# Hybrid decoder layer on one core: the weight tile's load issued ahead of the sum of w_ada and its load, in each step

## Chip, cores and metric

The kernel runs on 1 core of one Trainium2 chip. The metric is the device time of one execution in microseconds. Engines are PE (TensorE matmul, with PEld for its weight loads), DVE (VectorE), ACT (ScalarE), POOL (GpSimd) and SP (SyncE, which here issues all loads and stores, in one queue).

## What is computed

One decoder layer for x of 256 x 4096 in float32. Cut to what matters here:

```python
mod = jax.nn.silu(c) @ w_ada + b_ada             # c: 4096, w_ada: 4096 x 12288
shift, scale, gate = jnp.split(mod, 3, axis=-1)
h = rms_norm(x, norm_g) * (1 + scale[:, None, :]) + shift[:, None, :]
z = h @ w_in                                      # w_in: 4096 x 15520
...
yA = rms_norm(yA, out_norm_a_g) * jax.nn.silu(gA)
yB = rms_norm(yB, out_norm_b_g) * jax.nn.silu(gB)
y = jnp.concatenate([yA, yB], axis=-1) @ w_out    # w_out: 4096 x 4096
return x + gate[:, None, :] * y
```

Between the two products stand a spatial gating branch (yA) and a sparse attention branch (yB), both fed from z.

## The kernel before

**Steps.** All of `w_in` and `w_out` passes through one list, `stream`, of 624 steps. A step is a weight tile of 2 x 128 rows and mostly 512 columns (512 KB, name `raw`). For each step `load_w` (L400) issues the tile's load on SP, three steps ahead (`AHEAD` = 3) into one of four buffers (`WBUFS` = 4). `split` (L412) then cuts the tile into a high half `whi`, written by ACT (L419), and the rest `wlo` = raw - whi, of whose 1024 columns POOL writes 704 (L427, in two pieces) and DVE 320 (L425). `multiply` (L430) issues 10 or 12 matmuls of 512 columns (L457). A buffer of `raw` is free when ACT, POOL and DVE have read it.

**Chunks.** The rows of `w_in` come in eight chunks of 512, 46 steps each, for the columns in `early`: steps 0 to 367. After them come the columns of the two gate paths (128 steps) and `w_out` (128 steps). At the end of each visit of two steps DVE adds the product to what is there (`add_to`, L829), 1024 elements wide.

**The sums of w_ada.** A chunk can be multiplied only once h is known for its rows, and h needs scale and shift: `silu(c) @ w_ada`. The first chunk's share is made before step 0 (`first_ada`). The other seven are made beside the steps: `ada_gemv` (L181) takes a tile `wa` of 128 x 1024 (512 KB), multiplies it by a column of silu(c) and adds it to `acc` on DVE (L196, L194 for the first of a chunk), and then calls `load_ada` (L165), which issues the load of the next tile (L178) into the one of two `wa` buffers that this sum has just freed. `pace` (L1016) says in how many steps such a sum stands: it spreads the 33 turns of a chunk (32 sums, and one that hands `acc` to ACT) evenly over the columns that PE has to multiply until the chunk is due. It is called in steps 0 to 321 alone; in later steps sums of w_ada for the gate come from `tick` (called inside `step`, L463).

**Order.** The program runs under `manual_schedule`: each engine gets its instructions in the order in which the loop writes them. In a step t below 322 that is: `pace` (DVE's sum, then SP's `wa` load, which waits for it), then `step`: SP's load of the weight tile of step t + 3, `split`, the reading of products, `tick`, `multiply`.

Of the kernel before, what the change touches and what calls it, by code (L numbers as in the profile page):

```python
# [37 lines left out]
AHEAD = 3  # L38
# [4 lines left out]
def layer(ctx, tc, x, c, w_ada, b_ada, norm_g, w_in, ln_v_g, ln_v_b, w_s, b_s, q_norm_g,  # L43
# [25 lines left out]
    def flush():  # L69
        while pending:  # L70
            pending.pop(0)()
# [290 lines left out]
    def tick():  # L362
        small_ones[0] = 0
        for b in list(beside):
            b[2] += b[1]
        for b in list(beside):
            if small_ones[0] > 1:
                break
            again = False
            while b[2] >= 1.0:  # L370
                b[2] -= 1.0
                if again:
                    flush()
                again = True
                if next(b[0], "end") == "end":
                    beside.remove(b)
                    break
# [22 lines left out]
    def load_w(t):  # L400
        if t >= len(stream) or t in raws:
            return
        v, i = stream[t]
        nk, w, c0 = min(2, len(v["ks"]) - i), v["w"], v["c0"]
        raw = wp.tile([P, 2, 512], F32, name="raw")
        raw = raw[:, :nk]
        nc.sync.dma_start(raw[:, :, :w], v["src"][:, v["ks"][i]:v["ks"][i] + nk, c0:c0 + w])
        raws[t] = raw
# [3 lines left out]
    def split(t):  # L412

        raw, w = raws.pop(t), stream[t][0]["w"]
        nk = raw.shape[1]
        hi = [sp.tile([P, 512], F32R, name="whi") for _ in range(nk)]
        lo = [sp.tile([P, 512], F32R, name="wlo") for _ in range(nk)]
        for kk in range(nk):
            nc.scalar.activation(hi[kk][:, :w], raw[:, kk, :w], AF.Copy)  # L419
        left = nk * pool_cols[0] * w // 1024 * 2  # L420
        for kk in range(nk):
            cut = w - min(left, w)
            left -= w - cut
            if cut:
                nc.vector.tensor_sub(lo[kk][:, :cut], raw[:, kk, :cut], hi[kk][:, :cut].bitcast(F32))  # L425
            if cut < w:
                nc.gpsimd.tensor_sub(lo[kk][:, cut:w], raw[:, kk, cut:w], hi[kk][:, cut:w].bitcast(F32))  # L427
        halves[t] = hi, lo

    def multiply(t):  # L430

        v, i = stream[t]
        hi, lo = halves.pop(t)
        if i == 0:
            if v is visits[-1]:
                v["ps"] = [misc() for _ in range(NT)]
            else:
                both = mm.tile([P, NT, 512], F32, name="mm_ps", tag="mm")
                v["all"], v["ps"] = both, [both[:, n] for n in range(NT)]
        (ah, al), w, ks = v["parts"], v["w"], v["ks"][i:i + len(hi)]  # L440

        def half(a, k, n):
            return a[k][:, n * P:(n + 1) * P]
        todo = []
        for k, b in zip(ks, hi):
            if v["packed"]:
                todo += [(0, h_both[k], b), (1, half(ah, k, 1), b), (1, half(al, k, 1), b)]
            else:
                todo += [(n, half(a, k, n), b) for a in (ah, al) for n in range(NT)]
        for k, b in zip(ks, lo):  # L450
            todo += [(n, h_both[k] if v["packed"] and n == 0 else half(ah, k, n), b) for n in range(NT)]
        if t + 1 == len(stream):
            todo.sort(key=lambda x: x[0])
        ends = {n: max(j for j, x in enumerate(todo) if x[0] == n) for n in range(NT)}
        begun = set() if i == 0 else {0, 1}
        for j, (n, a, b) in enumerate(todo):
            nc.tensor.matmul(v["ps"][n][:, :w], a, b[:, :w], start=n not in begun,  # L457
                             stop=i + len(hi) == len(v["ks"]) and j == ends[n])
            begun.add(n)
# [1 line left out]
    reads = []  # L461

    def step(t):  # L463
        load_w(t + AHEAD)
        due = [v for u, v in reads if u <= t]
        del reads[:len(due)]
        split(t)
        flush()
        for v in due:
            v["read"](v)  # L470
        v, i = stream[t]
        if i == 0 and v["before"]:
            v["before"]()
        tick()
        multiply(t)
        if i + 2 >= len(v["ks"]):
            reads.append((t + 2, v))
# [538 lines left out]
    def pace(t):  # L1016
        nonlocal steps, owed
        cols = until[t + 1] - until[t]
        owed += max([((KC + 1) * b - steps) * cols / max(until[max(at[b] - LEAD, 0)] - until[t], cols)
                     for b in range(1, len(BLOCKS)) if (KC + 1) * b > steps] + [0.0])  # L1020
        while owed >= 1.0:
            owed -= 1.0
            steps += 1
            next(hs, None)
# [37 lines left out]
    with tc.manual_schedule():  # L1062
        for t in range(len(stream)):
            for begin in start.get(t, ()):
                begin()
            if t < last:
                pace(t)
            elif t == last:
                pool_cols[0] = POOL_REST
            step(t)  # L1070
        for _, v in reads:
            v["read"](v)
# [42 lines left out]
```

## Time and profile before

| | |
|---|---|
| median of 3 runs | 1890.69 us (1889.44 to 1894.2) |
| the profiled execution | 1893.78 us, its span 1892.1 us |
| granted TensorE clock over the span | 0.994 |
| PE matmul busy | 1809.0 us (96%) |
| PE weight loads busy | 1439.2 us (76%) |
| DVE busy | 1443.7 us (76%) |
| ACT busy | 933.4 us (49%) |
| POOL busy | 1299.2 us (69%) |
| moved by DMA | 542.53 MB, mean 287 GB/s |

Busy times are of one profiled execution. A matmul is drawn from its start to a modelled end, and the next one starts before that end, so PE's busy time is not the time that it needs. SP only issues and waits; its instructions are not counted as busy. Idle time of an engine is put down to what ended it.

### The profile page before, as it was taken

How to read it: one execution, taken by the hardware profiler on the slowest of the kernel's cores; microseconds unless marked ns; L12 is line 12 of the kernel's file. 1: busy time of each engine (PE TensorE's matmuls, PEld its weight loads, DVE VectorE, ACT ScalarE, POOL GpSimd, SP SyncE). 2: the span in 40 equal slices, each digit the busy share in tenths (PEclk: the TensorE clock that was granted, in tenths of full speed). 3: DMA queues.
4: the chain of work that ended last, by engine and by line, in shares of the span. 5: the costliest groups of instructions: out<-in, count | busy, mean ns of one | idle time of the engine just before them, and what ended most of it. 6: DMA issues, size and time to landing. Idle time of an engine off the chain costs nothing.

```text
span 1892.1 us, 27366 instructions
## 1 busy us (share of the span) xinstructions
PE 1809.0 (96%) x8100; PEld 1439.2 (76%) x8100; DVE 1443.7 (76%) x1600; ACT 933.4 (49%) x1716; POOL 1299.2 (69%) x1340
## 2 busy tenths in 40 slices
PE   5798999999999999999999999999999999999998
PEld 2476777777777777787788877788888888888877
DVE  4656788888888888888777888887887577677744
ACT  4356445445454354444455556567654554544443
POOL 0366777777777776777785545767667777877786
PEclk9899999999999999999999999999999999999999
DMA  9899999999999989999975467886788799899974
GB/s 319 316 340 323 314 317 316 318 324 309 341 320 333 319 300 315 329 301 322 311 210 152 132 206 257 267 264 202 245 281 303 248 332 339 294 318 343 320 216 154
DMA packets 269550, 542.53 MB, mean 287 GB/s; under 512 B 17270, under 2 KB 25688, under 8 KB 269404
## 3 DMA queue, kind: packets, MB, share of 16 engines
q1 hardware_dynamic: 269404, 540.79, 84.5%
q8 instruction: 66, 1.08, 0.2%
q14 instruction: 80, 0.66, 0.1%
HBM read 536.51 MB, written 4.22 MB: 286 GB/s over the span
## 4 chain that ended last, share of the span: by engine, by line
PE 45%; DVE 2%; DMA 1%; POOL 1%; ACT 1%; issue 1%; SPq 0%; DVEq 0%; POOLq 0%; ACTq 0%
PE mm_ps L457 38%; PE ms_ps L457 2%; PE ms_ps L573 1%; DMA raw<-in_w_in_dram 1%; DVE wlo L425 1%; PE ms_ps L714 0%; DVE acc L196 0%; POOL wlo L427 0%; PE ms_ps L915 0%; PE ms_ps L867 0%; DVE v L809 0%; PE ms_ps L556 0%; PE ms_ps L742 0%; ACT whi L419 0%; DVE ix L585 0%
## 5 line engine op out<-in xcount | busy, mean ns | idle before, releaser
L427 POOL TENSOR_TENSOR wlo<-raw,whi 128x512 fp32r<-128x512 f32 (+1 forms) x1248 | 1220.8, 1004 | 543.8 <-ACT whi L419 467.0
L419 ACT ACTIVATE whi<-raw 128x512 fp32r<-128x512 f32 (+1 forms) x1248 | 730.9, 618 | 829.9 <-DMA raw<-in_w_in_dram 385.1
L425 DVE TENSOR_TENSOR wlo<-raw,whi 128x320 fp32r<-128x320 f32 (+2 forms) x624 | 636.7, 1022 | 317.3 <-ACT whi L419 200.9
L457 PE MATMUL mm_ps<-whi,hh 128*128 128x512 f32 (+1 forms) x1728 | 566.2, 397 | 19.2 <-ACT whi L419 15.5
L457 PE MATMUL mm_ps<-whi,hl 128*128 128x512 f32 (+1 forms) x1728 | 550.7, 388 | 2.6 <-DVE hl L311 2.6
L457 PE MATMUL mm_ps<-wlo,hh 128*128 128x512 f32 (+1 forms) x1728 | 494.0, 388 | 14.3 <-DVE wlo L425 12.2
L196 DVE SCALAR_TENSOR_TENSOR acc<-wa,csil,acc 128x1024 f32<-128x1024 f32 x341 | 436.4, 1280 | 72.3 <-DMA wa<-in_w_ada_dram 71.2
L457 PEld LDWEIGHTS mm_ps<-whi,hh 128*128 128x128 f32 x1728 | 315.2, 190 | 97.2 <-ACT whi L419 31.0
L457 PEld LDWEIGHTS mm_ps<-wlo,hh 128*128 128x128 f32 x1728 | 320.4, 189 | 86.3 <-POOL wlo L427 12.0
L457 PEld LDWEIGHTS mm_ps<-whi,hl 128*128 128x128 f32 x1728 | 323.8, 189 | 71.0 <-DVE hl L311 2.9
L457 PE MATMUL mm_ps<-whi,yh 128*128 128x512 f32 x448 | 138.1, 389 | 0.0
L457 PE MATMUL mm_ps<-whi,yl 128*128 128x512 f32 x448 | 138.0, 389 | 0.0
L457 PE MATMUL mm_ps<-wlo,yh 128*128 128x512 f32 x448 | 120.2, 390 | 0.6 <-POOL wlo L427 0.6
L457 PE MATMUL mm_ps<-wlo,both 128*128 128x512 f32 x256 | 103.9, 406 | 4.3 <-DVE wlo L425 3.0
L457 PE MATMUL mm_ps<-whi,both 128*128 128x512 f32 x256 | 103.8, 405 | 3.9 <-ACT whi L419 2.8
L457 PEld LDWEIGHTS mm_ps<-wlo,yh 128*128 128x128 f32 x448 | 83.9, 188 | 19.0 <-POOL wlo L427 1.8
L457 PEld LDWEIGHTS mm_ps<-whi,yl 128*128 128x128 f32 x448 | 84.1, 188 | 17.6
L457 PEld LDWEIGHTS mm_ps<-whi,yh 128*128 128x128 f32 x448 | 84.0, 188 | 17.6 <-ACT whi L419 0.2
L457 PEld LDWEIGHTS mm_ps<-wlo,both 128*128 128x128 f32 x256 | 48.0, 187 | 30.7 <-POOL wlo L427 14.5
L829 DVE TENSOR_TENSOR qi<-qi,mm_ps 128x1024 f32<-128x1024 f32 x56 | 67.6, 1207 | 0.0
L457 PEld LDWEIGHTS mm_ps<-whi,both 128*128 128x128 f32 x256 | 48.0, 188 | 23.9 <-ACT whi L419 11.1
L217 PE MATMUL acc<-wa,csil 128*1 128x512 f32 x64 | 28.4, 613 | 10.9 <-DMA wa<-in_w_ada_dram 10.9
(190 smaller groups left out, 1035.5 us busy)
## 6 DMA issues: line engine op xcount, KB each, us to landing
raw<-in_w_in_dram SPq DMA_DIRECT2D x480, 512.0 KB, 5.9
wa<-in_w_ada_dram SPq DMA_DIRECT2D x384, 512.0 KB, 5.0
raw<-in_w_out_dram SPq DMA_DIRECT2D x128, 512.0 KB, 6.0
xs<-in_x_dram SPq DMA_DIRECT2D x8, 512.0 KB, 5.5
xres<-in_x_dram SPq DMA_DIRECT2D x8, 512.0 KB, 7.3
out_dram<-yt SPq DMA_DIRECT2D x16, 256.0 KB, 3.1
raw<-in_w_in_dram SPq DMA_DIRECT2D x16, 160.0 KB, 5.1
wk<-rb_d SPq DMA_DIRECT2D x16, 128.0 KB, 5.6
```

Of the source, the lines that this page charges most:

```text
L196: nc.vector.scalar_tensor_tensor(dst, src, csil[:, k:k + 1], dst, op0=OP.mult, op1=OP.add)
L217: nc.tensor.matmul(acc[g:g + 1, s, :w], csil[:, k:k + 1], wt[:, s], start=i < 4, stop=i >= KC // 2 - 4)
L419: nc.scalar.activation(hi[kk][:, :w], raw[:, kk, :w], AF.Copy)
L425: nc.vector.tensor_sub(lo[kk][:, :cut], raw[:, kk, :cut], hi[kk][:, :cut].bitcast(F32))
L427: nc.gpsimd.tensor_sub(lo[kk][:, cut:w], raw[:, kk, cut:w], hi[kk][:, cut:w].bitcast(F32))
L457: nc.tensor.matmul(v["ps"][n][:, :w], a, b[:, :w], start=n not in begun, stop=i + len(hi) == len(v["ks"]) and j == ends[n])
L573: nc.tensor.matmul(dots[:q, a * S:(a + 1) * S], qt[:, (h0 + a) * q:(h0 + a + 1) * q], kiT[:, :S], start=True, stop=True)
L829: nc.vector.tensor_add(z, z, p)
```

## The change

The call of `load_w` moves out of `step` and into the loop, ahead of `pace`. In a step t the load of the weight tile of step t + 3 is now written before DVE's sum of w_ada and before the load into the buffer that the sum frees.

```diff
@@ def step(t):
-        load_w(t + AHEAD)
         due = [v for u, v in reads if u <= t]
@@ with tc.manual_schedule():
             for begin in start.get(t, ()):
                 begin()
+            load_w(t + AHEAD)
             if t < last:
                 pace(t)
```

SP's queue in steps 148 to 152, before. `raw` are weight tiles (L407), `wa` tiles of w_ada (L178); the numbers are the buffers' names in the build.

```order
L407 DMA raw_4341<-in_w_in_dram 128x2x512
L178 DMA wa_4366<-in_w_ada_dram 128x2x512
L407 DMA raw_4368<-in_w_in_dram 128x2x512
L178 DMA wa_4393<-in_w_ada_dram 128x2x512
L407 DMA raw_4395<-in_w_in_dram 128x2x512
L407 DMA raw_4417<-in_w_in_dram 128x2x512
L178 DMA wa_4440<-in_w_ada_dram 128x2x512
L407 DMA raw_4442<-in_w_in_dram 128x2x512
L178 DMA wa_4467<-in_w_ada_dram 128x2x512
L407 DMA raw_4469<-in_w_in_dram 128x2x512
```

Here each `wa` load stands ahead of the weight load of its step: raw_4395 comes behind wa_4393, which waits for a sum. The same place on SP with the change:

```order
L407 DMA raw_4341<-in_w_in_dram 128x2x512
L407 DMA raw_4365<-in_w_in_dram 128x2x512
L178 DMA wa_4368<-in_w_ada_dram 128x2x512
L407 DMA raw_4392<-in_w_in_dram 128x2x512
L178 DMA wa_4395<-in_w_ada_dram 128x2x512
L407 DMA raw_4417<-in_w_in_dram 128x2x512
L407 DMA raw_4439<-in_w_in_dram 128x2x512
L178 DMA wa_4442<-in_w_ada_dram 128x2x512
L407 DMA raw_4466<-in_w_in_dram 128x2x512
L178 DMA wa_4469<-in_w_ada_dram 128x2x512
```

Each weight load has moved ahead of its step's `wa` load: raw_4392 is the former raw_4395, and wa_4395 the former wa_4393. DVE's queue at the same place, before; the change leaves its order as it is.

```order
L425 TENSOR_TENSOR wlo_4373<-raw_4294,whi_4371 128x320
L829 TENSOR_TENSOR qi1_168<-qi1_168,mm_ps_4305 128x1024
L196 SCALAR_TENSOR_TENSOR acc_3834<-wa_4317,csil_160,acc_3834 128x1024
L425 TENSOR_TENSOR wlo_4400<-raw_4319,whi_4398 128x320
L425 TENSOR_TENSOR wlo_4422<-raw_4341,whi_4420 128x320
L829 TENSOR_TENSOR v2_177<-v2_177,mm_ps_4352 128x1024
L196 SCALAR_TENSOR_TENSOR acc_3834<-wa_4366,csil_160,acc_3834 128x1024
```

The subtraction that reads raw_4294 is DVE's last use of the buffer that raw_4395 goes into. The sum of wa_4317, two rows on, is what the load of wa_4393 waits for; before, raw_4395 stood behind that wait, and with the change it does not.

## Rows read from the trace of the kernel before

**Rows 1.** Busy by stretch: us, busy us (x) of PE PEld DVE ACT POOL, PEclk, DMA share, GB/s

```profile
64.00:206.00 142.00, 126.00 (x541) 100.23 (x542) 92.24 (x105) 79.82 (x132) 91.99 (x95) 0.95 0.90 311
206.00:962.00 756.00, 730.34 (x3212) 574.23 (x3211) 631.84 (x639) 342.65 (x620) 560.17 (x564) 1.00 0.92 316
...
1500.00:1600.00 100.00, 100.00 (x451) 82.98 (x450) 77.30 (x73) 46.74 (x81) 72.95 (x74) 1.00 0.93 324
```

**Rows 2.** The chain that ended last, 1500 to 1660: start us, us, what

```profile
1502.24 43.54 PE mm_ps L457 x192
```

**Rows 3.** PE's groups by shape, 206 to 962: xcount | busy us, mean ns | idle before

```profile
L457 PE MATMUL mm_ps<-whi,hh 128*128 128x512 f32 x864 | 287.6, 396 | 13.9 <-ACT whi L419 12.4 <-DVE u L829 0.4 <-DVE v L829 0.4
...
L457 PE MATMUL mm_ps<-whi,both 128*128 128x512 f32 x192 | 77.7, 405 | 3.9 <-ACT whi L419 2.8 <-DVE v L829 0.8
L263 PE MATMUL ms_ps<-one,accs 128*128 128x1 f32 x96 | 11.0, 245 | 0.0
...
L457 PE MATMUL mm_ps<-whi,hh 128*128 128x160 f32 x48 | 9.1, 270 | 0.0
```

**Rows 4.** Waits of ACT and of DVE, 206 to 962: total us, times, longest

```profile
ACT whi L419 <- DMA raw<-in_w_in_dram: 302.7, 155, 5.0
...
DVE wlo L425 <- ACT whi L419: 90.7, 99, 3.1
DVE acc L196 <- DMA wa<-in_w_ada_dram: 29.5, 35, 3.0
```

**Rows 5.** SP's own waits, 206 to 962: total us, times, longest

```profile
SPq L178 <- DVE acc L196: 264.4, 131, 4.5
SPq L178 <- DVE wlo L425: 111.4, 47, 4.2
SPq L178 <- DMA wa<-in_w_ada_dram: 78.2, 81, 3.8
...
SPq L407 <- POOL wlo L427: 30.8, 74, 1.2
```

**Rows 6.** DMA, 206 to 930: GB/s in 40 slices; loads, KB, median us to landing

```profile
GB/s 322 342 336 314 308 294 324 331 315 333 307 321 298 309 354 321 356 324 339 298 299 345 327 320 332 333 280 308 322 321 298 316 344 297 301 315 324 317 328 340
...
raw<-in_w_in_dram SPq DMA_DIRECT2D x254, 512.0 KB, 6.3
wa<-in_w_ada_dram SPq DMA_DIRECT2D x183, 512.0 KB, 5.3
```

**Rows 7.** Timeline at 490 us, SP, DVE, POOL, ACT: start us, us, what, idle before

```profile
491.67 0.37 SPq L178 DMA_DIRECT2D wa<-in_w_ada_dram  x1
492.13 0.93 SPq L407 DMA_DIRECT2D raw<-in_w_in_dram  x2
...
495.71 0.42 SPq L407 DMA_DIRECT2D raw<-in_w_in_dram  x1
...
489.24 1.21 DVE L829 TENSOR_TENSOR qi<-qi,mm_ps 128x1024 f32<-128x1024 f32 x1
490.37 1.27 DVE L196 SCALAR_TENSOR_TENSOR acc<-wa,csil,acc 128x1024 f32<-128x1024 f32 x1
...
493.94 1.28 DVE L196 SCALAR_TENSOR_TENSOR acc<-wa,csil,acc 128x1024 f32<-128x1024 f32 x1
...
487.67 2.10 POOL L427 TENSOR_TENSOR wlo<-raw,whi 128x512 fp32r<-128x512 f32 x2 [1.54 <-ACT whi L419]
490.44 6.24 POOL L427 TENSOR_TENSOR wlo<-raw,whi 128x512 fp32r<-128x512 f32 x6 [0.66 <-ACT whi L419]
...
489.73 2.44 ACT L419 ACTIVATE whi<-raw 128x512 fp32r<-128x512 f32 x4 [1.62 <-DMA raw<-in_w_in_dram]
...
497.95 2.45 ACT L419 ACTIVATE whi<-raw 128x512 fp32r<-128x512 f32 x4 [2.92 <-DMA raw<-in_w_in_dram]
```

**Rows 8.** First chunk, 64 to 206: DVE's waits; loads, KB, median us to landing

```profile
DVE acc L196 <- DMA wa<-in_w_ada_dram: 32.5, 26, 3.4
...
wa<-in_w_ada_dram SPq DMA_DIRECT2D x41, 512.0 KB, 4.5
```

## Prediction

> **What bounds the kernel now.** I cut the span where one part of the program ends and the next begins, because the change acts in one part alone: `pace` runs only in steps 0 to 321, which are seven chunks of 46 steps. The view of busy time by stretch comes first [rows 1]. The first chunk takes 142 us (64 to 206), the next six, 276 steps, 756 us (206 to 962). The reader should see that in those six no resource stands out: PE is busy 730 of 756 us, DVE 632, and the DMA engines 0.92 of the time.
>
> PE's busy figure hides loss, since each matmul is drawn longer than the distance to the next. That distance is read from an undisturbed stretch late in the kernel: 43.54 us for 192 matmuls, 0.2268 us each [rows 2]. Against it stands a drawn duration of 0.40 us [rows 3]. So I price PE's work by the distance. The 512-column matmuls of the six chunks (three kinds of 864, two of 192; one of each is shown) are 2976 x 0.2268 = 675 us. The 144 narrow ones (three kinds of 48) are drawn 0.27 us long; less the same tail of 0.17 us that is 0.10 us each, 15 us by estimate. The 96 small ones that sum the modulations are 11 us [rows 3]. PE's floor is 701 us, so **55 us, 9 us a chunk, are lost to waiting**. That is the whole prize in these six chunks.
>
> Who is late? The waits of the same stretch [rows 4]: ACT waited 302.7 us, 155 times, for the weight tile `raw`; DVE waited 90.7 us for ACT's half `whi`, and only 29.5 us for a `wa` tile. So the weight tile comes late and ACT late behind it, and what multiplies comes late behind ACT.
>
> Why is it late? SP's own waits say it [rows 5]: SP stood 264.4 + 111.4 + 78.2 = 454 us in front of the `wa` load (L178), against 30.8 us for POOL in front of the weight load (L407). Over 183 `wa` loads [rows 6] that is 2.5 us each, and the weight load stands behind in the same queue. The stretch at 490 us shows one case in full [rows 7]. POOL's pair that ends at 489.77 is the last reader of a weight buffer; nothing else keeps the next load. But DVE first does an addition of 1.21 us and then the sum of `wa` from 490.37 to 491.64; SP issues `wa` at 491.67 and the weight tile at 492.13, 2.36 us late. That tile is the one for which ACT then sits idle 2.92 us before 497.95. In the next case POOL's second pair after that is done at about 494.6 (490.44 plus two thirds of 6.24), the sum at 495.22, and the weight load goes out at 495.71, 1.1 us late: here the sum came before the addition could. So a weight load loses about 1.1 us, or 2.4 us where an addition stands between, in each step that has a sum.
>
> **The change part by part.** *Moved:* in steps 0 to 321 the weight load of step t+3 goes ahead of the sum, and so of the `wa` load, of step t. No instruction is added or removed, and DVE's order is the same. From step 322 on nothing stands between the old place and the new.
>
> *What the weight loop gains.* Four buffers make a loop of four steps: landing 6.3 us [rows 6], then the use of the tile (from ACT's start at 489.73 to POOL's end at 492.5, a third of the way through its six: 2.8 us [rows 7]), then the delay of the next issue. At 756/276 = 2.74 us a step the loop has 10.96 us; 6.3 + 2.8 leave 1.9 us for the delay and rests, which agrees with 1.1 to 2.4 us in two steps of three. Without the delay the loop is 9.1 us, 2.28 us a step, below PE's floor of 701/276 = 2.54 us. The weight loop then no longer sets the pace.
>
> *What is late next.* First PE itself, at 701 us. Second the DMA: it moved 316 GB/s on average in the six chunks [rows 1], in slices of 18 us between 280 and 356 [rows 6]. At PE's floor the same bytes need 316 x 756/701 = 341 GB/s, a rate that only the best slices have. Third DVE: 632 us of work and 29.5 us of waits for `wa` fit into 701 us, but closely.
>
> *The wait that is added.* SP now waits for the weight buffer (POOL's subtraction, above all) with the `wa` load queued behind, and DVE's sum waits for what that brings. In both cases of rows 7 POOL was done before the sum was (489.77 against 491.64, 494.6 against 495.22), so `wa` would go out when it does now. I take 0; the upper bound is what POOL's wait costs the weight load now, 30.8/74 = 0.4 us each [rows 5]. The loop of the two `wa` buffers is 5.3 us of landing [rows 6] and 1.3 us of sum [rows 7], 6.6 us for two loads, where 756 us and 183 loads give 8.3 us and PE's floor 7.7 us. Neither bound eats that room of 1.1 us.
>
> *The first chunk.* DVE waits 32.5 us for `wa` in its 142 us, more than in the six others together, with 41 loads [rows 8]. There the `wa` loop sets the pace, and an earlier weight tile brings little. I take 0, between 10 us gained (7%, as the six would at PE's floor) and the loss that the third rival prices.
>
> *Sum.* The six chunks can give 0 (the DMA holds its rate) to 55 us (PE's floor). I take 30, somewhat over half. The nearest stretch argues for the upper part: from 1500 to 1600 us, where a step's weight load already goes before its sum, PE is busy 100 of 100 us with the DMA at 324 GB/s [rows 1]. But PE's floor would need 5% more than that rate, and waits for `wa` grow with it. A gain of 30 us means 726 us at 329 GB/s. The profiled execution took 1893.8 us, so it becomes 1863.8; the median of the runs shown is 3.1 us lower, and I forecast **1861 us**.
>
> **The rivals.**
>
> *PE's floor is reached* (chance 0.17). All waits behind weights vanish, 55 us: 1836 us. For it speaks the late stretch; against it the rate of 341 GB/s.
>
> *Nothing moves* (0.13). The transfer is hidden anyway: the DMA engines are busy 0.92 of the time already, and a load issued 2 us sooner only lies longer in the queue; or its own buffer is the true gate and the change does not do what it says. Time 1891 us. Against it: slices of 345 and 356 GB/s in the same stretch [rows 6] show room, and rows 7 show the buffer free while SP stood elsewhere.
>
> *The `wa` tile becomes the late one* (0.08). Of two loads issued 0.46 us apart the second lands after 6.3 us and the first after 5.3 [rows 6, 7]: being second costs 1.0 us. If the two simply swap, the `wa` loop grows from 6.6 to 7.6 us for two. In the six chunks that is about PE's floor of 7.7, and since DVE does nothing else while it waits for a sum, I give them no gain. In the first chunk, which waits for `wa` already, 41 loads in two buffers lose 0.5 us each, 20 us: 1891 + 20 = 1911 us. It decides from the point at which `wa` lands 0.5 us or more later, 5.8 us, and the six chunks gain less than the first loses; beyond 7.0 us (8.3 less 1.3) the six lose too. What speaks against it is that the two loads would no longer be issued together: the weight load leaves 1 to 2.4 us before, and 512 KB at the 356 GB/s of the best slice are 1.5 us, so it is mostly through when `wa` comes.
>
> The Trainium skill ("DMA: Bandwidth & Descriptors", section "Queues, rings and completion order") states that on each DMA engine descriptors are consumed in ring order; by it alone the swap would be a full one and the time that of this last rival, 1911 us. The 1.0 us between first and second agrees with it.
>
> **How the numbers follow.** My forecast, a gain of 10 to 45 us, has 0.62; PE's floor 0.17, nothing 0.13, slower 0.08. The range reaches from PE's floor to a gain of 3 us, and leaves out the slower case and most of the case of nothing: 1836 to 1888 us. A measurement of this kernel can tell some 0.3%, 5.7 us, from no change. Faster by more: 0.79 (the two gaining cases); within it 0.13; slower 0.08.
>
> **What the profile after would show.** The weight load of a step is issued right behind POOL's subtraction, 1 to 2.4 us ahead of the `wa` load. In the six chunks ACT's waits for `raw` fall from 302.7 to under 200 us, some of them turning into waits for PE to free `whi`; the chunks take about 726 us at some 329 GB/s; `wa` lands in 5.3 to 6 us, and DVE's waits for it grow from 29.5 to at most 60 us. The first chunk stays within 5 us of 142, and all after step 322 keeps its length. I am wrong in the mechanism if ACT's waits for `raw` fall and the six chunks still take over 746 us, and wrong on the side if the first chunk grows by more than the six others lose.

## Result and profile after

The changed kernel takes 1842.81 us (1841.71 to 1843.71, 4 runs) against 1891.62 us before. The ratio is 0.9741 with a 95% interval of 0.9724 to 0.9758: 49 us or 2.6% faster, inside the range and larger than the 30 us forecast.

Busy time by stretch of the changed kernel, cut at the same steps (0, 46, 322, end); columns as in [rows 1].

```profile
64.00:201.00 137.00, 122.98 (x533) 98.41 (x534) 87.07 (x103) 80.82 (x131) 88.99 (x94) 0.95 0.92 320
201.00:912.00 711.00, 706.90 (x3219) 583.60 (x3218) 589.15 (x641) 360.95 (x621) 554.12 (x566) 1.00 0.96 336
912.00:1842.00 930.00, 914.24 (x4222) 752.50 (x4220) 691.80 (x824) 491.67 (x938) 645.95 (x673) 1.00 0.77 256
```

The six chunks fell from 756 to 711 us, 45 us; the first chunk from 142 to 137; what follows step 322 took 930 us before (1892 less 962) and after. So the whole gain lies in the 322 steps that the change touches. The six chunks are now 10 us above PE's floor of 701.

The waits in the six chunks, ACT's, DVE's and SP's own; they answer to [rows 4, 5].

```profile
ACT whi L419 <- PE mm_ps L457: 134.1, 184, 2.9
ACT whi L419 <- POOL wlo L427: 93.4, 84, 1.9
ACT whi L419 <- DMA raw<-in_w_in_dram: 86.0, 58, 3.2
...
DVE acc L196 <- DMA wa<-in_w_ada_dram: 78.0, 67, 3.3
DVE wlo L425 <- ACT whi L419: 36.9, 41, 2.0
...
SPq L407 <- DVE wlo L425: 162.9, 159, 3.3
SPq L178 <- DVE wlo L425: 139.2, 84, 2.5
SPq L178 <- DVE acc L196: 106.8, 95, 3.0
SPq L178 <- DMA wa<-in_w_ada_dram: 63.9, 53, 3.9
SPq L407 <- POOL wlo L427: 53.4, 130, 1.5
```

ACT's waits for the weight tile went from 302.7 to 86.0 us, and ACT now waits most for PE to give `whi` buffers back: it runs ahead of PE. SP still stands 310 us in front of the `wa` load, but no weight load behind it could go at once: the next one waits for a subtraction that DVE makes only after that same sum. SP's waits in front of the weight load (L407), 216 us, are for the buffer itself. DVE waits more for `wa`, 78.0 us against 29.5.

SP and DVE at the place of [rows 7] in the changed kernel (timeline; start us, us).

```profile
466.72 0.37 SPq L178 DMA_DIRECT2D wa<-in_w_ada_dram  x1
467.19 0.41 SPq L407 DMA_DIRECT2D raw<-in_w_in_dram  x1
469.45 0.37 SPq L178 DMA_DIRECT2D wa<-in_w_ada_dram  x1
...
466.61 0.48 DVE L425 TENSOR_TENSOR wlo<-raw,whi 128x320 fp32r<-128x320 f32 x1
467.01 1.21 DVE L828 TENSOR_TENSOR qi<-qi,mm_ps 128x1024 f32<-128x1024 f32 x1
468.14 1.28 DVE L196 SCALAR_TENSOR_TENSOR acc<-wa,csil,acc 128x1024 f32<-128x1024 f32 x1
```

DVE's subtraction, the last reader of the buffer, ends at 467.09 and the weight load goes out at 467.19. The sum ends at 469.42 and the `wa` load goes at 469.45, 2.3 us behind, where before the weight load would have stood.

The DMA in 201 to 880 us of the changed kernel; columns as in [rows 6].

```profile
GB/s 360 346 360 369 319 330 302 364 363 342 365 338 314 311 372 329 358 385 331 319 299 375 317 372 381 331 323 287 349 359 341 386 357 303 291 335 331 344 360 355
...
raw<-in_w_in_dram SPq DMA_DIRECT2D x254, 512.0 KB, 5.8
wa<-in_w_ada_dram SPq DMA_DIRECT2D x184, 512.0 KB, 5.3
```

The weight tile lands in 5.8 us instead of 6.3, and `wa` in 5.3 as before. The two kinds of loads are not spread out, though: of the 184 `wa` loads of the six chunks, 139 still have a weight load within 1 us behind them (183 of 183 before), now the one of the next step, as at 466.72 and 467.19. What has become rare is two weight loads within 1 us of each other, 10 instead of 50.

How late a weight load goes out can be read from the traces for every step from 50 to 321: from the end of the last subtraction that reads its buffer to its own start, 1.44 us on average before and 0.06 us in the changed kernel.

### The profile page after: what moved, and what is told of

Its sections match the earlier page's. It is cut to its first block, busy times and chain, and to the rows that moved or that the text cites. A ratio compares the mean times of both kernels' runs of the same rounds, so it can differ in the third digit from the quotient of the medians.

```text
span 1842.0 us, 27366 instructions
## 1 busy us (share of the span) xinstructions
PE 1782.3 (97%) x8100; PEld 1446.0 (79%) x8100; DVE 1397.0 (76%) x1600; ACT 953.5 (52%) x1716; POOL 1291.0 (70%) x1340
## 5 line engine op out<-in xcount | busy, mean ns | idle before, releaser
L419 ACT ACTIVATE whi<-raw 128x512 fp32r<-128x512 f32 (+1 forms) x1248 | 748.8, 621 | 743.6 <-PE mm_ps L457 266.1
L425 DVE TENSOR_TENSOR wlo<-raw,whi 128x320 fp32r<-128x320 f32 (+2 forms) x624 | 592.2, 952 | 262.8 <-ACT whi L419 152.2
L196 DVE SCALAR_TENSOR_TENSOR acc<-wa,csil,acc 128x1024 f32<-128x1024 f32 x341 | 436.9, 1281 | 125.2 <-DMA wa<-in_w_ada_dram 124.1
```

What stands on the lines that cost most here:

```text
L196: nc.vector.scalar_tensor_tensor(dst, src, csil[:, k:k + 1], dst, op0=OP.mult, op1=OP.add)
```

## Experiments

Each ratio is against the kernel before in the same series: 1890.7 us for `old_order_wa3`, `old_order_raw5`, `new_order_raw5` and `new_order_wa3`, 1895.7 us for the other four. Times of different series are therefore compared by their ratios.

Theory A: what cost time was SP's stand in front of the `wa` load, with the weight load behind it. Rivals were B, the place in the queue; F, the `wa` tiles; G, the DMA's rate. Three more concern what is left after the change: C, weights still late; D, `wa` tiles late; E, the DMA full.

**The old order with most of the stand gone.** A third `wa` buffer, in memory that is free until the last chunk's h is made (`hh28`). Loads stay two tiles ahead, so each goes into a buffer that was freed one sum earlier.

```diff
+THIRD = 190
...
+    all_ada = list(ada_loads)
...
+        n = len(all_ada) - len(ada_loads)
...
-            wt = wp.tile([P, per, ns, width], F32, name="wa", tag="wa", bufs=2)
+            wt = (hp.tile([P, per, ns, width], F32, name="wa", tag="hh28") if n % 3 == 2 and n < THIRD else
+                  wp.tile([P, per, ns, width], F32, name="wa", tag="wa", bufs=2))
```

> The old order, with a third buffer for w_ada tiles that is used only to free a buffer one sum earlier: still two tiles ahead, the weight load still written behind the w_ada load, but that load no longer waits for the sum of its own step. Theory A (what cost time is that SP stands in front of the w_ada load until the sum is done, and the weight load stands behind it, 1.1 to 2.4 us in two steps of three): the stand goes without any instruction changing its place, so the six chunks fall from 756 us to about 711 as in the changed kernel, and the time to 1838 to 1850 us. Rival B (what counts is the place in the queue: a weight tile right behind a w_ada tile lands 1 us later): each weight load still follows a w_ada load, so at most 10 us are gained, 1880 to 1891 us.

1833.93 us, ratio 0.9694 (0.9659 to 0.9729): the gain comes without any load changing its place in the order, and it is somewhat larger than A said. B falls: it allowed 10 us at most. The stand is not all gone: where the third buffer is in use throughout, SP still waits 49.0 + 28.6 + 3.0 = 81 us in front of the `wa` load (323 in the same four chunks before), but over steps 50 to 321 the weight load goes out 0.32 us behind the last reader of its buffer on average, instead of 1.44. The four chunks that have the third buffer throughout run at PE's floor (4 x 117 = 468 us):

```profile
194.00:663.00 469.00, 469.00 (x2148) 390.65 (x2147) 420.71 (x431) 244.53 (x415) 378.20 (x378) 1.00 0.97 344
```

This run moves the `wa` tiles forward too, so it does not yet separate A from F. The next one does.

**The same three buffers, with the stand.** One more edit: three tiles ahead, so that a load waits again for its own step's sum.

```diff
-        if ada_loads:
...
+        if ada_loads and len(ada_tiles) < (3 if n < THIRD else 2):
...
     load_ada()
     load_ada()
+    load_ada()
```

> The old order with the same third w_ada buffer, but loading three tiles ahead, so that the w_ada load of a step again waits for that step's own sum. Beside the run with two tiles ahead it brings back SP's stand alone; the w_ada tiles come as early as there or earlier. Theory A: the weight loads are late again, ACT's waits for them in the six chunks come back to about 300 us, the chunks to 740 to 756 us, and the time to 1870 to 1890 us. Rival F (the third buffer itself helped there, because DVE stopped waiting for w_ada tiles, and the weights' lead matters little): as with two ahead, 1828 to 1840 us.

1881.25 us, ratio 0.9936 (0.9902 to 0.9971). Its six chunks by stretch (lines of this kernel are 4 further down than before):

```profile
192.00:948.00 756.00, 729.93 (x3212) 575.97 (x3211) 638.35 (x639) 342.80 (x620) 564.14 (x564) 1.00 0.92 315
```

The waits of ACT and DVE and SP's own in that stretch:

```profile
ACT whi L423 <- DMA raw<-in_w_in_dram: 296.8, 150, 4.5
...
DVE acc L200 <- DMA wa<-in_w_ada_dram: 4.9, 6, 1.9
...
SPq L182 <- DVE acc L200: 316.6, 141, 5.4
```

This is the strongest of the runs. The six chunks take 756 us, the time of the kernel before, and ACT waits 296.8 us for weights, as before, although DVE hardly waits for `wa` at all. The weight load is late again, by 1.29 us on average. So the `wa` tiles were not what held the old kernel's six chunks: F falls, A stands.

The weight tile's landing moves with the stand too: 6.3 us in this run, 5.7 in the run before it. That is 0.6 us of the loop beside 1.0 us of delay (1.29 against 0.32), and no run changes one without the other while the buffers are four. So it is shown that the stand cost the time, but how its cost divides between late issue and slower landing is only estimated: of the old loop of 10.96 us, taking off the delay that the change removes (1.44 less 0.06) leaves 2.40 us a step, below PE's 2.54, and taking off the landing alone (6.3 less 5.8) leaves 2.62, above it.

What this kernel does gain is in its first chunk, 130 us (62 to 192) instead of 142.

**The old order with a fifth weight buffer**, in the same free memory, in steps 0 to 285.

```diff
+DEEP = 290
...
-        raw = wp.tile([P, 2, 512], F32, name="raw")
+        raw = (hp.tile([P, 2, 512], F32, name="raw", tag="hh28") if t % 5 == 4 and t < DEEP else
+               wp.tile([P, 2, 512], F32, name="raw"))
...
-        load_w(t + AHEAD)
+        load_w(t + (4 if t + 4 < DEEP else AHEAD))
...
-    for t in range(AHEAD):
+    for t in range(4):
```

> The old order, with a fifth buffer for weight tiles and loads four steps ahead, in steps 0 to 286. Theory A: the delay of 1.1 to 2.4 us stays, but the loop of weight buffers has five steps for its 11 us, 2.2 us a step, below PE's 2.54, so nearly all of the gain comes back: 1840 to 1855 us. SP stands in front of the w_ada load as long as before. Rival B: the order of the two loads is as before, so the time is too, 1883 to 1891 us.

1846.28 us, ratio 0.9764 (0.9734 to 0.9793), as A said. The six chunks (195 to 914) take 719 us. SP's stand is still there, 181.9 + 159.6 + 124.1 us in them, the weight load goes out 1.85 us late and its tile lands in 6.2 us; the longer loop covers both:

```profile
SPq L179 <- DVE wlo L427: 181.9, 83, 3.9
SPq L179 <- DVE acc L197: 159.6, 96, 4.6
SPq L179 <- DMA wa<-in_w_ada_dram: 124.1, 110, 3.0
```

**The changed order with three weight buffers** (WBUFS 3, AHEAD 2), which tests the loop's arithmetic.

```diff
-WBUFS = 4
+WBUFS = 3
-AHEAD = 3
+AHEAD = 2
```

> The changed order with three weight buffers instead of four and loads two steps ahead, in the whole kernel. Theory A, the loop of weight buffers in numbers: landing 5.8, use 2.8, delay 0.1, 8.7 us for three steps, 2.9 us a step, 800 us for the 276 steps of the six chunks (711 with four buffers). Later parts lose as well, by less where steps are longer. Time 1920 to 1990 us. Rival G (the loop is not what binds, the DMA's rate is): 711 to 730 us in the six chunks.

2015.2 us, ratio 1.0628 (1.0592 to 1.0664). The total is outside what was expected, since the parts after step 322 lost more than I allowed (1015 us instead of 930) and step 0 began 13 us later (77 against 64). The six chunks, for which there was a number, took 786 us against 800 from the loop and 711 to 730 from G:

```profile
216.00:1002.00 786.00, 741.69 (x3209) 569.76 (x3208) 641.23 (x640) 342.80 (x620) 562.09 (x565) 1.00 0.91 303
```

786/276 x 3 is 8.5 us for the loop. Of these the landing is 5.2 us here (median), not the 5.8 that I put in, so 3.3 us are left for use and delay instead of 2.9: the figure of 800 came within 2% by two errors of opposite sign, which is luck. The trace of this run has 3.1 us of use and 0.05 us of delay on average. The dependence on the number of buffers is shown. G falls: the rate is lower than before, 303 GB/s, with PE waiting.

**The changed order with a fifth weight buffer** (the edit above on the changed kernel).

> The changed order with the same fifth weight buffer. Theory A: with the delay gone the loop of four buffers (5.8 us landing + 2.8 + 0.1 = 8.7 us, 2.2 us a step) no longer sets the pace, so a fifth one gives at most 4 us: 1838 to 1844 us. Rival C (ACT's remaining waits for weights, 86 us in the six chunks, still cost): 8 us or more are gained, 1835 us or less.

1850.1 us, ratio 0.9782 (0.9752 to 0.9813): neither theory's time, some 7 us above the changed kernel, whose interval (0.9724 to 0.9758) it barely touches. Waits in its six chunks:

```profile
ACT whi L421 <- DMA raw<-in_w_in_dram: 21.4, 15, 3.3
...
DVE acc L197 <- DMA wa<-in_w_ada_dram: 90.4, 77, 3.0
```

ACT's waits for weights went from 86.0 to 21.4 us and nothing was gained, so C falls. DVE's waits for `wa` grew from 78.0 to 90.4 us, and the six chunks took 717 us. That a weight load sent still earlier takes its rate from the `wa` tile fits this; no run tests it by itself.

**The changed order with a third `wa` buffer** and three tiles ahead (the first two edits on the changed kernel).

> The changed order with a third buffer for w_ada tiles, and three of them ahead, for the first 190 of them. Theory D (what is left of PE's loss, some 10 us in the six chunks and more in the first, comes from DVE's waits for w_ada tiles, 78 and 39 us): these waits fall to under 30 us together, the first chunk by 5 to 10 us and the six by 5 to 10: 1823 to 1835 us. Rival E (the DMA is full at a share of 0.96 and 336 GB/s): a third tile ahead only lies longer in the queue and takes from the weights: 1839 to 1848 us.

1825.58 us, ratio 0.9653 (0.9624 to 0.9681). DVE's waits for `wa` are 16.8 us in the six chunks and 2.3 in the first, the six take 704 us (191 to 895) and the first 126: D stands, E falls. **The same for 222 tiles instead of 190:**

> The changed order with the third w_ada buffer kept for 222 tiles instead of 190, which is until just before its memory is needed for the last chunk's h. Theory D: the last of the six chunks comes down from 119 us to the 117 of the others, 2 to 4 us in all: 1821 to 1824 us. If DVE's waits for w_ada tiles are not what is left there, nothing: 1825 to 1826 us.

1820.63 us, ratio 0.9606 (0.9582 to 0.963), slightly beyond what was expected and the lowest ratio of all, 75 us below the kernel before in its series. Against the run with 190 tiles the intervals touch, and the six chunks differ by 2 us (702 and 704). Its first chunk and its six chunks by stretch:

```profile
63.00:191.00 128.00, 121.63 (x537) 101.93 (x537) 106.36 (x105) 83.37 (x132) 96.72 (x95) 0.93 0.96 350
191.00:893.00 702.00, 702.00 (x3217) 584.78 (x3215) 625.16 (x639) 366.18 (x619) 566.21 (x565) 1.00 0.97 339
```

DVE's waits for `wa` in the six:

```profile
DVE acc L200 <- DMA wa<-in_w_ada_dram: 2.8, 4, 1.4
```

PE is busy 702.00 of 702 us, on the floor of 701 that the prediction worked out from the distance of matmuls. Three tiles ahead for the first 190 tiles are worth some 17 us in the changed order (ratio 0.9741 to 0.9653) and 12 in the old one (1 to 0.9936), there nearly all in the first chunk: the third buffer reaches the six chunks only where the weights are in time.

**The changed order from step 46 on.** The edit is against the kernel before, and the old call in `step` stays; `load_w` does nothing for a tile that has been loaded.

```diff
+            if t >= 46:
+                load_w(t + AHEAD)
             if t < last:
                 pace(t)
```

> The weight load first from step 46 on only; in the first chunk the old order. Theory A with additive parts: the first chunk keeps its 142 us and the six take 711, so 1847 us (1844 to 1850), the changed kernel's time plus the first chunk's 5 us. Rival: the first chunk's 5 us are chance of one profile, and the time is the changed kernel's, 1843 us or less.

1845.52 us (1842.09 to 1848.56), ratio 0.9728 (0.9697 to 0.9759), the ratio of the changed kernel, so the time does not tell whether the first chunk's 5 us are real. The profile, of the slowest of its four runs, does lean that way: the first chunk is back at 141 us (62 to 203) and the six take 714.

## Why the prediction was right, and what it sized wrong

*Why the weights were late.* Right, and shown: with the same buffers, the stand moves the six chunks between 756 us and 716 (194 to 910 in the run with most of it gone, whose last chunks lack the third buffer). The loop of four buffers was the right picture too: a fifth buffer in the old order does what the change does, and one fewer in the new order undoes it. Its terms were read from a single case and were some tenths off: over steps 50 to 321 of the old trace the use of a tile is 3.1 us and not 2.8, and the delay 1.4 us of the 1.9 that were left for it and the rests.

*The sum, "I take 30, somewhat over half".* This is the term that was off. The six chunks gave 45 of 55 us, and the whole kernel 49: more than the 10 to 45 us to which I gave 0.62, and closer to the rival in which PE's floor is reached (55 us, 0.17). The range held it only because it reached down to that rival. I held back because of the DMA: PE's floor needed 341 GB/s, "a rate that only the best slices have". The changed kernel moved 336 GB/s over all six chunks, the fastest one 339, and the old order with three `wa` buffers 344 over four chunks. The rates that I read in the old trace were what the loads asked for, not what the DMA could do. The waits for `wa` did grow, but not with the rate as I said: in the fastest kernel, at 339 GB/s, they are 2.8 us.

*DVE "fits closely".* It does not bind: in the fastest kernel DVE is busy 625 of 702 us and PE does not wait.

*The added wait.* Right in its price, but the working left out a row. In front of the weight load SP waited longer for DVE than for POOL already before:

```profile
SPq L407 <- DVE wlo L425: 53.8, 41, 3.4
```

In the changed kernel DVE's subtraction is the main wait there, 162.9 us against 53.4 for POOL, and not "POOL's subtraction, above all". It costs the `wa` load nothing, since DVE makes that subtraction before the sum that frees the `wa` buffer: 183 of the 184 `wa` loads of the six chunks go out within 0.3 us of that sum's end.

The third rival did not come about, for the reason given there: of the 183 `wa` loads that follow a weight load, 175 go out more than 1 us behind it, and `wa` lands in 5.3 us as before. The rule cited from the Trainium skill ("DMA: Bandwidth & Descriptors", "Queues, rings and completion order") is not contradicted, but with the weight load 1 to 2 us ahead it leaves little to queue behind; by it alone 1911 us had been named, and 1843 was measured.

*DVE's waits for `wa`* were to stay below 60 us and reached 78. The added wait is not the cause: in the old order with five weight buffers they are 71.3 us. What failed is the sum of the `wa` loop, 6.6 us of 7.7, "room of 1.1 us". It takes the sums as evenly spaced, and they are not: they stand in about two steps of three, and 41 of the 185 in the six chunks fall two steps after the sum that freed their buffer. By estimate two steps (5.1 us) less a sum (1.3 us) leave 3.8 us for a landing of 5.3. In the trace these 41 have 52.5 of the 78.0 us. That is the next limit, as the third buffer shows, and I had it as a thing to watch, not as what is late next.

*The first chunk.* I took 0 and the profile shows 5 us; with the third `wa` buffer it falls to 126 to 130 us, so that it was bound by the `wa` loop in good part was right. *After step 322* nothing moved, as said.

## What to carry to other kernels

In a queue that issues loads for two consumers, a load that must wait for a computation holds up those behind it that could go at once; write first the load whose buffer comes free first. What that is worth is read from the loop of buffers, (landing + use + delay of the next issue) / buffers, against the work of the engine it feeds. When one loop is relieved, work out the next one before buying buffers, and by the shortest distance of its steps, not their mean: here a fifth weight buffer brought nothing on top of the new order, and a third one for the other stream, whose loop had room by the mean, brought some 17 us.

## What the runs showed of the hardware that was not expected

**The DMA holds for 50 us a rate that the old trace has only in short slices.** In the old trace's first chunk the slices of 3.6 us reach 381 GB/s, and one of 2.5 us between 1500 and 1600 us has 409. In the first chunk of the fastest kernel the slices of 3.2 us read:

```profile
GB/s 262 337 360 298 2 303 351 215 367 379 390 383 368 389 387 390 396 399 409 410 406 408 408 408 409 411 397 390 387 360 378 405 403 378 314 383 259 345 157 210
```

For 16 slices, some 51 us, it holds 387 to 411 GB/s, while SP issues w_in and w_ada loads of 512 KB in turn.

**DVE's subtraction takes 0.48 or 1.17 us, by what POOL does.** In the six chunks of the changed kernel the 47 subtractions of 320 columns that start while POOL runs nothing take 0.48 to 0.49 us each, the other 218 from 0.48 to 1.65. The mean fell from 944 ns to 778. DVE's group of 320 columns, by shape, in the kernel before:

```profile
L425 DVE TENSOR_TENSOR wlo<-raw,whi 128x320 fp32r<-128x320 f32 x264 | 249.0, 944 | 92.0 <-ACT whi L419 88.6 <-PE mm_ps L457 2.4
```

The same group in the changed kernel:

```profile
L425 DVE TENSOR_TENSOR wlo<-raw,whi 128x320 fp32r<-128x320 f32 x265 | 205.4, 778 | 33.8 <-ACT whi L419 29.8 <-PE mm_ps L457 3.9
```

In the timeline of the kernel before, POOL starts a pair at 362.13:

```profile
362.13 2.12 POOL L427 TENSOR_TENSOR wlo<-raw,whi 128x512 fp32r<-128x512 f32 x2 [2.06 <-PE mm_ps L457]
```

DVE's subtraction, in the same timeline, starts 0.48 us into it and takes 1.17 us:

```profile
362.61 1.17 DVE L425 TENSOR_TENSOR wlo<-raw,whi 128x320 fp32r<-128x320 f32 x1 [1.80 <-ACT whi L419]
```

In the changed kernel the one at 466.61, shown above, takes 0.48 us; POOL's next pair starts only at 467.17:

```profile
467.17 1.86 POOL L427 TENSOR_TENSOR wlo<-raw,whi 128x512 fp32r<-128x512 f32 x2 [1.21 <-ACT whi L419]
```

The Trainium skill ("SBUF — State Buffer", section "Who interferes with whom") says that a DVE instruction with two inputs in SBUF contends with a GpSimd instruction that reads SBUF, and that the ports they share are an exclusive lock; the two durations agree with it. The mean is low where DVE waits long for `wa` (778 ns with 78.0 us of such waits) and high where it does not (923 ns with 2.8 us in the fastest kernel), so the subtraction seems to fall clear of POOL's pieces when DVE runs late; no run tests this. The 44 us of busy time saved are no cause of the gain, since the fastest kernel has DVE at 625 us again.
